# Sums and splits of activations made one stage earlier and kept in DRAM

## Chip, cores and metric

The kernel runs on one core of a Trainium2 chip. The metric is the time of one execution in device microseconds (us); the median of several runs is compared. One execution of each kernel is also recorded by the hardware profiler, and all rows below come from such a record.

## What is computed

The reference is one layer of a flow-matching backbone on 1024 latent tokens and 128 context tokens, 1024 wide. Two parallel mixers come first; the change lies in the channel mixer behind them:

```python
h2 = rmsnorm(x, p["norm2_g"]) * (1.0 + scale2) + shift2
ff = (jax.nn.silu(h2 @ p["w_ffn_gate"]) * (h2 @ p["w_ffn_up"])) @ p["w_ffn_down"]
x = x + gate2 * ff
...
y_prompt = rmsnorm(xp, final_norm_g)
y_sample = rmsnorm(xs, final_norm_g)
```

The hidden width is 2816, that is 22 tiles of 128. The kernel works in float32: each operand of a matmul is split in a high part (a cast to float32r) and a low part (the rest), and a product is the three matmuls high*high, high*low, low*high.

## The kernel before

**Gate and up stage.** A unit (`ffn_unit`) makes the gate (kind "g") or up (kind "u") product of two of the 22 hidden tiles; units g and u of number p belong together (a pair of units, p = 0 to 10). Seven products replace eight (a scheme of Strassen's kind): sums of weight blocks are made on POOL (L1172 to L1174, L1188), each is split by `split` (copy on ACT, L962; low part on POOL, L963), and PE multiplies it with prepared activations TA and TB (L1149). The tokens are two groups, A with five tiles and B with four. PSUM results are combined by ACT and DVE, gate and up are multiplied, and the hidden activations go to the DRAM tensor `ffd` (L1207). Unit 0 runs for group A first, alone, and for group B after pair 2.

**Down stage.** It multiplies the hidden activations (now the contraction) with w_down. Hidden tiles 2m and 2m+1 form tile m, 0 to 10. Block 0 is m = 0, four blocks take m in pairs (1,2) to (7,8), and the last (`std_block`) takes 9 and 10. Blocks up to m = 8 use the seven-product scheme with KEYS P1 to P7; `std_block` makes plain products. For each m the weights (`wd`, L1332) and the raw activations (`fr`, L1318; `raw0` for m = 0) are loaded. `prep` (called once per key) forms sums of them in place (`sub`, L1346, on POOL) and splits both: BT from the weights, AT from the activations (`split2`: copy on ACT, L1308; low part on DVE or POOL, L1309). `prep_std` does it for 9 and 10 without sums. Products are made by `prods` (L1387) into four PSUM banks Z, W, X, Y, which are added to the accumulator ACC by DVE (L1406; the first time copied by ACT, L1404). A bank is used again when it has been added. The prompt's parts (`load_p`, pr, P) go their own way. Prepared A tiles sit in a ring of NA = 10 buffers, raw ones in NFR = 6; `feed` prepares the next key as `step` counts keys as used, up to FA = 10 ahead. At the end come the gate, the residual (`gate_x`, x1), the squares and the final norm.

**Order.** All DMAs are issued by the queue of SP, in one order. The order on each engine is not that of the program text: a scheduler with a simulated timeline takes each instruction as its inputs and buffers are due, and the text's order decides between those that are ready. So the loads and first splits of `raw0`, written behind the loop of units, run in the midst of it (at 907 us). On the chip each engine, and SP's queue, goes strictly in the order so fixed, and a waiting instruction holds all behind it. The pools pA (A tiles, raw tiles) and px (ACC) lie in memory that TA and TB hold until the last gate and up product.

Of the kernel before, what the change touches and what calls it, by code (L numbers as in the profile page):

```python
# [19 lines left out]
NS = 1024  # L20
# [29 lines left out]
NA = 10  # L50
NFR = 6
# [10 lines left out]
def tile_flow_step(ctx: ExitStack, tc: tile.TileContext, a, o):  # L62
# [25 lines left out]
    def f32(ap):  # L88
        return ap.bitcast(F32)
# [1173 lines left out]
    open_sub("B", {z: ps2 for z in "ZWXY"}, pm0, "m0a")  # L1263
    for p in range(1, NF // 2):
        ffn_unit(p, "g", "AB")
        ffn_unit(p, "u", "AB")
        if p == 2:
            ffn_unit(0, "g", "B")
            ffn_unit(0, "u", "B")

# [7 lines left out]
    BLK = [[0]] + [[m, m + 1] for m in range(1, 9, 2)]  # L1278
    STD = [9, 10]
    KEYS = ("P1", "P2", "P6", "P5", "P7", "P4", "P3")  # L1280
# [3 lines left out]
    LO, HI = slice(0, 512), slice(512, 1024)  # L1284
    A0 = pm0.tile([128, 3, 2, 512], F32R, tag="m0b", name="A0")
    raw0 = pgb.tile([128, 2, NS], F32, tag="gb", name="raw0")
# [14 lines left out]
    def a_new(name):  # L1301
        return pA.tile([128, 2, 512], F32R, tag="A", bufs=NA, name=name)

    def b_new(name):
        return ringed("b", [128, 2, 512], F32R, "wh", NWH, "R", NR, name)
# [5 lines left out]

    def load_a(m):
        if m in araw:
            return
        araw[m] = []
        for f in range(2):
            t_ = raw0[:, f] if m == 0 else pA.tile([128, NS], F32, tag="fr", bufs=NFR, name=f"fr{2 * m + f}")
            SY.dma_start(out=t_, in_=ffd[2 * m + f][:, 0:NS])  # L1318
            araw[m].append(t_)
# [15 lines left out]
    def load_raw(m):  # L1335
        load_w(m)
        load_a(m)
        raws[m] = [x[:, h] for x in wraw[m] + araw[m] for h in (LO, HI)]
# [6 lines left out]
    def sub(out, x, y, op=ALU.subtract, eng=None):  # L1345
        (eng or PL).tensor_tensor(out, x, y, op)  # L1346

    def prep(m, ki):
        key = KEYS[ki]
        w0L, w0H, w1L, w1H, a0L, a0H, a1L, a1H = raws[m]  # L1350
        if key == "P6":
            sub(a0H, a0H, a1H, ALU.add)
            sub(w0H, w1H, w0H, eng=V if m in VSUB else PL)
            sub(a0L, a0H, a0L)
            sub(w0L, w0H, w0L, ALU.add, V if m in VSUB else PL)
        if key == "P7":
            sub(a1L, a1L, a0L)
            sub(a0L, a1H, a0L)
        if key == "P5":
            sub(w1L, w1L, w0L)  # L1360
            sub(w0L, w1H, w0L)
        asrc, bsrc = dict(P1=(a0L, w0L), P2=(a1L, w1L), P6=(a0L, w0L), P7=(a0L, w0H),
                          P4=(a1H, w1L), P5=(a0H, w0L), P3=(a1L, w1H))[key]
        if m == 0:
            A = A0[:, ki] if ki < 3 else a_new(f"A0{key}")
            B = wr.tile([128, 2, 512], F32R, tag="wh" if ki < 6 else "ftA", bufs=NWH if ki < 6 else 1, name=f"B0{key}")
        else:
            A, B = a_new(f"A{m}{key}"), b_new(f"B{m}{key}")
        BT[m, key] = split2(B, bsrc, PL if m == 0 else V)
        AT[m, key] = split2(A, asrc, PL if m > 0 and key in ("P2", "P7") else V)  # L1370

    def prep_std(m, ki):
        w0L, w0H, w1L, w1H, a0L, a0H, a1L, a1H = raws[m]
        for (i, j, asrc), (k, n, bsrc) in (
                (((1, 0, a0H), (0, 0, w0L)), ((1, 1, a1H), (1, 0, w1L)),
                 ((0, 0, a0L), (0, 1, w0H)), ((0, 1, a1L), (1, 1, w1H)))[ki],):
            BT[m, (k, n)] = split2(b_new(f"B{m}{k}{n}"), bsrc, V)
            AT[m, (i, j)] = split2(a_new(f"A{m}{i}{j}"), asrc, PL)
# [222 lines left out]
    for m in BLK[1]:  # L1601
        load_a(m)
# [124 lines left out]
```

## Time and profile before

| | us |
|---|---|
| median of 3 runs | 1538.99 (1536.73 to 1542.13) |
| the profiled execution | 1546.39 |
| its span | 1544.3 |
| PE busy in it | 1470.2 (95%) |
| DVE, ACT, POOL busy | 900.0, 568.5, 721.4 |

Times in rows count from the start of the span. Busy time of PE is time in which some matmul is in its pipeline; a matmul's own length (0.39 us for 512 columns) is longer than the distance to the next one. The gate and up stage with both groups runs from about 793 us, the down stage from 1256.5 us, and the last matmul ends at 1527.3 us.

### The profile page before, as it was taken

The numbers are of one execution on the slowest core, as the hardware profiler recorded it, in microseconds if no ns is written. First come the engines' busy times: TensorE is split into PE (matmuls) and PEld (weight loads), VectorE is DVE, ScalarE is ACT, GpSimd is POOL, SyncE is SP. The second block draws the span as 40 slices with busy tenths as digits, with TensorE's granted clock in tenths as the row PEclk, the third lists the DMA queues.
The fourth block names the chain that finished last, engine by engine and source line by source line (L and its number), as shares of the span: only waits on it lengthen the run. The fifth ranks groups of instructions, "written<-read, shape, count | busy, mean of one in ns | idle before, by whom it ended". The sixth has DMA issues, their size and how long they took to land.

```text
span 1544.3 us, 23785 instructions
## 1 busy us (share of the span) xinstructions
PE 1470.2 (95%) x8999; PEld 1317.4 (85%) x8999; DVE 900.0 (58%) x1786; ACT 568.5 (37%) x1096; POOL 721.4 (47%) x658
## 2 busy tenths in 40 slices
PE   6999999999989999998899999999999998999995
PEld 3799998989968779777679999999999997777774
DVE  4557989997255335379952432222222259989978
ACT  6433243343454121354532343232333244333323
POOL 4920000000022111354688679777777785775454
PEclk9999999999989999999899999999999999999998
DMA  8333233232525653455532122221222255222313
GB/s 310 117 124 96 74 109 97 83 111 91 179 66 177 210 160 113 136 205 176 178 114 86 56 99 86 86 78 44 79 86 73 72 182 185 97 85 86 105 52 123
DMA packets 84703, 180.91 MB, mean 117 GB/s; under 512 B 13790, under 2 KB 44127, under 8 KB 84588
## 3 DMA queue, kind: packets, MB, share of 16 engines
q1 hardware_dynamic: 84588, 179.38, 35.1%
q8 instruction: 71, 1.16, 0.3%
q14 instruction: 44, 0.36, 0.1%
HBM read 141.05 MB, written 38.28 MB: 116 GB/s over the span
## 4 chain that ended last, share of the span: by engine, by line
PE 58%; DVE 11%; issue 2%; DMA 2%; POOL 2%; ACT 1%; SPq 0%; DVEq 0%; ACTq 0%; POOLq 0%
PE U L1387 4%; PE p L106 2%; PE p L105 2%; PE p L104 2%; DVE acc L1406 2%; PE ada L155 1%; DVE wh_out L963 1%; PE V L1387 1%; PE o L978 1%; PE o L979 1%; PE o L977 1%; DVE acc L1485 1%; DMA wd<-in_w_d 1%; PE g L272 1%; PE g L273 1%
## 5 line engine op out<-in xcount | busy, mean ns | idle before, releaser
L94 POOL TENSOR_TENSOR wh_glu<-ws_glu,wh_glu 128x512 fp32r<-128x512 f32 x4 | 5.5, 1388 | 340.3 <-ACT wh_glu L93 340.3
L272 PE MATMUL g<-h,wh_g 128*128 128x384 f32 (+1 forms) x432 | 148.0, 343 | 0.0
L271 PE MATMUL g<-h,wh_g 128*128 128x384 f32 (+1 forms) x432 | 148.0, 342 | 0.0
L273 PE MATMUL g<-h,wh_g 128*128 128x384 f32 (+1 forms) x432 | 147.4, 341 | 0.0
L271 PEld LDWEIGHTS g<-h,wh_g 128*128 128x128 f32 x432 | 82.0, 190 | 0.3 <-issue 0.3
L272 PEld LDWEIGHTS g<-h,wh_g 128*128 128x128 f32 x432 | 82.0, 190 | 0.2 <-issue 0.2
L273 PEld LDWEIGHTS g<-h,wh_g 128*128 128x128 f32 x432 | 82.0, 190 | 0.2 <-issue 0.2
L94 POOL TENSOR_TENSOR wh_pj<-ws_pj,wh_pj 128x512 fp32r<-128x512 f32 x16 | 22.1, 1380 | 103.8 <-ACT wh_pj L93 94.2
L963 DVE TENSOR_TENSOR wh_out<-ws_out,wh_out 128x512 fp32r<-128x512 f32 x32 | 33.8, 1072 | 24.6 <-ACT wh_out L962 24.6
L1346 POOL TENSOR_TENSOR wd<-wd,wd 128x512 f32<-128x512 f32 x25 | 37.7, 1517 | 21.7 <-DMA wd<-in_w_d 10.8
L1387 PE MATMUL q<-B,A 128*128 128x512 f32 x192 | 45.7, 394 | 1.1 <-DVE acc L1406 0.9
L963 POOL TENSOR_TENSOR wh_out<-ws_out,wh_out 128x512 fp32r<-128x512 f32 x16 | 21.8, 1371 | 50.6 <-ACT wh_out L962 47.6
L1387 PEld LDWEIGHTS q<-B,A 128*128 128x128 f32 x192 | 35.9, 188 | 10.1 <-DVE acc L1406 1.3
L1406 DVE TENSOR_TENSOR acc<-acc,U 128x1024 f32<-128x1024 f32 x34 | 41.1, 1213 | 2.0 <-PE U L1387 1.6
L923 DVE TENSOR_TENSOR sgc<-sgc,p 128x384 f32<-128x384 f32 x24 | 13.3, 555 | 48.4 <-PE p L106 48.4
L977 PE MATMUL o<-wh_out,m 128*128 128x512 f32 x96 | 36.6, 409 | 4.6 <-ACT scr0b L1059 4.6
L636 DVE TENSOR_TENSOR ta<-X,Sg 128x56 f32<-128x56 f32 (+10 forms) x88 | 39.5, 449 | 1.1
L639 DVE TENSOR_TENSOR X<-X,tb 128x56 f32<-128x56 f32 (+10 forms) x88 | 39.4, 455 | 0.9
L1166 ACT ACTIVATE fsA<-ftA 128x320 f32<-128x320 f32 x33 | 15.6, 471 | 65.4 <-DVE ftA L1185 39.9
L962 ACT CAST wh_out<-ws_out 128x512 fp32r<-128x512 f32 x48 | 28.3, 615 | 30.1 <-PE o L979 20.3
L1346 POOL TENSOR_TENSOR fr<-fr,fr 128x512 f32<-128x512 f32 x24 | 37.4, 1571 | 4.3 <-DMA fr<-ffd 4.3
L978 PE MATMUL o<-wh_out,m 128*128 128x512 f32 x96 | 38.5, 403 | 0.7 <-DVE wh_out L963 0.7
(1664 smaller groups left out, 4600.0 us busy)
## 6 DMA issues: line engine op xcount, KB each, us to landing
wa<-in_w_ada SPq DMA_DIRECT2D x48, 512.0 KB, 5.7
ws_out<-in_w_out SPq DMA_DIRECT2D x24, 512.0 KB, 3.9
wd<-in_w_d SPq DMA_DIRECT2D x22, 512.0 KB, 8.1
ind<-in SPq DMA_DIRECT2D x54, 192.0 KB, 1.9
fr<-ffd SPq DMA_DIRECT2D x20, 512.0 KB, 4.9
ws_g<-in_w_in SPq DMA_DIRECT2D x18, 512.0 KB, 3.5
sgc<-ind SPq DMA_DIRECT2D x48, 192.0 KB, 3.5
ffd<-fsA SPq DMA_DIRECT2D x11, 640.0 KB, 3.1
```

Of the source, the lines that this page charges most:

```text
L104: PE.matmul(ps, w[:, 0, wsl], act[:, 0][asl], start=first, stop=False)
L271: PE.matmul(ps, w[:, 0, wsl], hi, start=first, stop=False)
L272: PE.matmul(ps, w[:, 0, wsl], lo, start=False, stop=False)
L273: PE.matmul(ps, w[:, 1, wsl], hi, start=False, stop=last)
L636: V.tensor_tensor(A, src, Sc[:, 0, lv, gs].unsqueeze(1).unsqueeze(3).to_broadcast(shp), ALU.mult)
L639: V.tensor_tensor(dst, dst, B[:, ::-1], ALU.add)
L963: (eng or PL).tensor_tensor(w[:, 1, :], src, f32(w[:, 0, :]), ALU.subtract)
L977: PE.matmul(p, mc[t][0][:, k, ts_], w[n][:, 0], start=(k == 0), stop=False)
L978: PE.matmul(p, mc[t][0][:, k, ts_], w[n][:, 1], start=False, stop=False)
L1346: (eng or PL).tensor_tensor(out, x, y, op)
L1387: PE.matmul(ps, A[:, va], B[:, vb], start=(first and ti == 0 and i == 0), stop=(last and ti == n - 1 and i == 2), skip_group_check=True)
L1406: V.tensor_tensor(dst, dst, ps, ALU.add)
```

## The change

For tiles m = 0 to 9 the sums and splits of activations are made inside the gate and up stage. `a_steps(m)` loads the two raw tiles back from `ffd` into the buffer "gb" (ra), makes for each key the sums on DVE, the copy of the high part on ACT and the low part on DVE into one of three staging buffers (`stg`, in the buffer "m0b"), and stores both parts to a DRAM tensor `ad[m]`. The steps are handed to the units as hooks, one after each product. Tile 10 stays as it was. In the down stage `load_at` loads a prepared tile of 512 KB from `ad`; `prep` and `prep_std` now prepare only the weights (and tile 10). Five tiles of m = 0 go to buffers that `stg` and `ra` held (A0, A1). The ring of A tiles grows from 10 to 12, that of raw tiles shrinks from 6 to 4. Sums that POOL made are now made by DVE, and so are the low parts that POOL made (P2, P7 and tile 9).

```diff
--- before.py
+++ after.py
@@ -47,8 +47,8 @@
 XBG = 1
 NWA = 4
 NR = 4
-NA = 10
-NFR = 6
+NA = 12
+NFR = 4
 NW2 = 3
 NPT = 2
 NXR = 2
@@ -1261,12 +1261,64 @@
     pst_.release()
     ps2 = open_pool("psF2", space=PSUM)
     open_sub("B", {z: ps2 for z in "ZWXY"}, pm0, "m0a")
+    KEYS = ("P1", "P2", "P6", "P5", "P7", "P4", "P3")
+    LO, HI = slice(0, 512), slice(512, 1024)
+    BLK = [[0]] + [[m, m + 1] for m in range(1, 9, 2)]
+    STD = [9, 10]
+    ad = {m: dram.tile([7 if m < STD[0] else 4, 128, 2, 512], F32, tag=f"ad{m}", name=f"ad{m}")
+          for m in range(STD[1])}
+    stg = pm0.tile([128, 3, 2, 512], F32R, tag="m0b", name="stg")
+    nstg = 0
+
+    def a_steps(m):
+        box = {}
+
+        def start():
+            raw = pgb.tile([128, 2, NS], F32, tag="gb", name=f"ra{m}")
+            for f in range(2):
+                SY.dma_start(out=raw[:, f], in_=ffd[2 * m + f][:, 0:NS])
+            box["a"] = [raw[:, f, h] for f in range(2) for h in (LO, HI)]
+
+        def one(ki):
+            nonlocal nstg
+            a0L, a0H, a1L, a1H = box["a"]
+            if m >= STD[0]:
+                src = (a0H, a1H, a0L, a1L)[ki]
+            else:
+                key = KEYS[ki]
+                if key == "P6":
+                    V.tensor_tensor(a0H, a0H, a1H, ALU.add)
+                    V.tensor_tensor(a0L, a0H, a0L, ALU.subtract)
+                if key == "P7":
+                    V.tensor_tensor(a1L, a1L, a0L, ALU.subtract)
+                    V.tensor_tensor(a0L, a1H, a0L, ALU.subtract)
+                src = dict(P1=a0L, P2=a1L, P6=a0L, P7=a0L, P4=a1H, P5=a0H, P3=a1L)[key]
+            st_ = stg[:, nstg % 3]
+            nstg += 1
+            S.copy(out=st_[:, 0], in_=src)
+            V.tensor_tensor(st_[:, 1], src, f32(st_[:, 0]), ALU.subtract)
+            SY.dma_start(out=ad[m][ki], in_=f32(st_))
+
+        n = 7 if m < STD[0] else 4
+        return [start, no, no] + [lambda ki=ki: one(ki) for ki in range(n)]
+
+    apend = []
+
+    def anext():
+        if apend:
+            apend.pop(0)()
+
     for p in range(1, NF // 2):
-        ffn_unit(p, "g", "AB")
-        ffn_unit(p, "u", "AB")
+        for kind in "gu":
+            ffn_unit(p, kind, "AB", [anext] * 7)
         if p == 2:
             ffn_unit(0, "g", "B")
             ffn_unit(0, "u", "B")
+            apend += a_steps(2) + a_steps(0)
+        elif p < STD[1]:
+            apend += a_steps(p)
+    while apend:
+        anext()
 
 
     ps2.release()
@@ -1275,15 +1327,11 @@
     pTA.release()
     pT.release()
     psp = open_pool("psC", space=PSUM)
-    BLK = [[0]] + [[m, m + 1] for m in range(1, 9, 2)]
-    STD = [9, 10]
-    KEYS = ("P1", "P2", "P6", "P5", "P7", "P4", "P3")
     px = open_pool("px")
     ACC = px.tile([128, 9, D], F32, tag="acc", name="acc")
     pA = open_pool("pA")
-    LO, HI = slice(0, 512), slice(512, 1024)
     A0 = pm0.tile([128, 3, 2, 512], F32R, tag="m0b", name="A0")
-    raw0 = pgb.tile([128, 2, NS], F32, tag="gb", name="raw0")
+    A1 = pgb.tile([128, 2, 2, 512], F32R, tag="gb", name="A1")
     ring = dict(b=0, w=0)
     AT, BT, PT, raws, araw, wraw = {}, {}, {}, {}, {}, {}
     pR = pE = pW = None
@@ -1309,12 +1357,17 @@
         (eng or V).tensor_tensor(w[:, 1], src, f32(w[:, 0]), ALU.subtract)
         return w
 
+    def load_at(m, ki):
+        key = KEYS[ki] if m < STD[0] else ((1, 0), (1, 1), (0, 0), (0, 1))[ki]
+        if (m, key) in AT:
+            return
+        AT[m, key] = (A0[:, ki] if ki < 3 else A1[:, ki - 3]) if m == 0 and ki < 5 else a_new(f"A{m}_{ki}")
+        SY.dma_start(out=f32(AT[m, key]), in_=ad[m][ki])
+
     def load_a(m):
-        if m in araw:
-            return
         araw[m] = []
         for f in range(2):
-            t_ = raw0[:, f] if m == 0 else pA.tile([128, NS], F32, tag="fr", bufs=NFR, name=f"fr{2 * m + f}")
+            t_ = pA.tile([128, NS], F32, tag="fr", bufs=NFR, name=f"fr{2 * m + f}")
             SY.dma_start(out=t_, in_=ffd[2 * m + f][:, 0:NS])
             araw[m].append(t_)
 
@@ -1334,8 +1387,9 @@
 
     def load_raw(m):
         load_w(m)
-        load_a(m)
-        raws[m] = [x[:, h] for x in wraw[m] + araw[m] for h in (LO, HI)]
+        if m == STD[1]:
+            load_a(m)
+        raws[m] = [x[:, h] for x in wraw[m] + araw.get(m, []) for h in (LO, HI)]
 
     def load_p(m):
         pr = pA.tile([128, 2, 128], F32, tag="pr", bufs=2, name=f"pr{m}")
@@ -1347,35 +1401,31 @@
 
     def prep(m, ki):
         key = KEYS[ki]
-        w0L, w0H, w1L, w1H, a0L, a0H, a1L, a1H = raws[m]
+        w0L, w0H, w1L, w1H = raws[m]
         if key == "P6":
-            sub(a0H, a0H, a1H, ALU.add)
             sub(w0H, w1H, w0H, eng=V if m in VSUB else PL)
-            sub(a0L, a0H, a0L)
             sub(w0L, w0H, w0L, ALU.add, V if m in VSUB else PL)
-        if key == "P7":
-            sub(a1L, a1L, a0L)
-            sub(a0L, a1H, a0L)
         if key == "P5":
             sub(w1L, w1L, w0L)
             sub(w0L, w1H, w0L)
-        asrc, bsrc = dict(P1=(a0L, w0L), P2=(a1L, w1L), P6=(a0L, w0L), P7=(a0L, w0H),
-                          P4=(a1H, w1L), P5=(a0H, w0L), P3=(a1L, w1H))[key]
+        bsrc = dict(P1=w0L, P2=w1L, P6=w0L, P7=w0H, P4=w1L, P5=w0L, P3=w1H)[key]
         if m == 0:
-            A = A0[:, ki] if ki < 3 else a_new(f"A0{key}")
             B = wr.tile([128, 2, 512], F32R, tag="wh" if ki < 6 else "ftA", bufs=NWH if ki < 6 else 1, name=f"B0{key}")
         else:
-            A, B = a_new(f"A{m}{key}"), b_new(f"B{m}{key}")
+            B = b_new(f"B{m}{key}")
+        load_at(m, ki)
         BT[m, key] = split2(B, bsrc, PL if m == 0 else V)
-        AT[m, key] = split2(A, asrc, PL if m > 0 and key in ("P2", "P7") else V)
 
     def prep_std(m, ki):
-        w0L, w0H, w1L, w1H, a0L, a0H, a1L, a1H = raws[m]
-        for (i, j, asrc), (k, n, bsrc) in (
-                (((1, 0, a0H), (0, 0, w0L)), ((1, 1, a1H), (1, 0, w1L)),
-                 ((0, 0, a0L), (0, 1, w0H)), ((0, 1, a1L), (1, 1, w1H)))[ki],):
-            BT[m, (k, n)] = split2(b_new(f"B{m}{k}{n}"), bsrc, V)
-            AT[m, (i, j)] = split2(a_new(f"A{m}{i}{j}"), asrc, PL)
+        w0L, w0H, w1L, w1H = raws[m][0:4]
+        (k, n), bsrc = (((0, 0), w0L), ((1, 0), w1L), ((0, 1), w0H), ((1, 1), w1H))[ki]
+        if m == STD[1]:
+            a0L, a0H, a1L, a1H = raws[m][4:8]
+            ij, asrc = (((1, 0), a0H), ((1, 1), a1H), ((0, 0), a0L), ((0, 1), a1L))[ki]
+            AT[m, ij] = split2(a_new(f"A{m}_{ki}"), asrc, PL)
+        else:
+            load_at(m, ki)
+        BT[m, (k, n)] = split2(b_new(f"B{m}{k}{n}"), bsrc, V)
 
     def bank(z, name):
         return psp.tile([128, 2, 512], F32, tag=z, name=name)
@@ -1598,8 +1648,9 @@
     for ki in range(7):
         prep(0, ki)
     load_w(1)
-    for m in BLK[1]:
-        load_a(m)
+    for ki in range(4):
+        for m in BLK[1]:
+            load_at(m, ki)
     load_p(0)
     for st_ in last_st:
         SY.dma_start(**st_)
```

## Rows read from the trace of the kernel before

**Rows 1.** Stages: stretch, length, busy us (count) of PE, PEld, DVE, ACT, POOL, clock...
```profile
850.00:1256.50 406.50, 406.50 (x3099) 406.50 (x3099) 105.92 (x220) 125.46 (x252) 305.00 (x260) 1.00 0.22 75
...
1256.50:1527.30 270.80, 257.12 (x1085) 203.92 (x1083) 247.30 (x249) 102.66 (x192) 167.16 (x103) 0.99 0.34 117
...
1527.30:1544.30 17.00, 0.00 (x0) 0.00 (x0) 11.97 (x29) 5.62 (x15) 5.22 (x4) 0.64 0.38 153
```

**Rows 2.** PE alone in a stretch of the down stage without a gap.
```profile
1338.50:1363.50 25.00, 25.00 (x110) 1.00 0.43 153
```

**Rows 3.** Waits of PE, 1240 to 1545: total us, times, longest; 11 rows.
```profile
PE Zp L1387 <- DVE acc L1406: 3.4, 4, 1.4
...
PE V L1387 <- DVE acc L1406: 2.5, 1, 2.5
...
PE Y L1387 <- DVE B1P L1309: 1.6, 1, 1.6
```

**Rows 4.** PE's timeline after a wait: start, length, instruction, count, idle before.
```profile
1466.89 1.29 PE L1387 MATMUL V<-B7P,A7P 128*128 128x512 f32 x3 [2.49 <-DVE acc L1406]
...
1471.32 0.86 PE L1387 MATMUL U<-B7P,A7P 128*128 128x512 f32 x3
```

**Rows 5.** Chain of waits in the down stage: start, length, what.
```profile
1323.10 0.60 DVE A3P L1309
...
1323.70 1.70 DVE A4P L1309
...
1330.88 1.70 DVE A4P L1309
...
1333.76 3.06 PE Zp L1387 x12
...
1376.87 1.79 POOL fr L1346 x2
...
1382.31 1.27 DVE B5P L1309
```

**Rows 6.** Raw activations fr, 1256.5 to 1480: busy us (count) of DVE, ACT, POOL.
```profile
1256.50:1480.00 223.50, 40.33 (x40) 38.93 (x64) 87.74 (x56) 0.98 0.38 130
```

**Rows 7.** Timeline of DVE and POOL where both have work.
```profile
1412.41 1.75 POOL L1346 TENSOR_TENSOR fr<-fr 128x512 f32<-128x512 f32 x1
...
1412.92 1.78 DVE L1309 TENSOR_TENSOR A8P<-fr,A8P 128x512 fp32r<-128x512 f32 x1
...
1414.11 1.74 POOL L1346 TENSOR_TENSOR wd<-wd 128x512 f32<-128x512 f32 x1
```

**Rows 8.** All engines, 1266 to 1276; the last number is GB/s.
```profile
1266.00:1276.00 10.00, 9.07 (x40) 7.14 (x38) 10.00 (x9) 8.54 (x15) 10.00 (x7) 1.00 1.04 412
```

**Rows 9.** Timeline of POOL before unit g3 and before unit g9.
```profile
898.05 1.29 POOL L1172 TENSOR_TENSOR s_g3AB<-ws_g3AB 128x512 f32<-128x512 f32 x1 [1.39 <-DMA ws_g3AB<-in_w_g]
...
904.00 2.54 POOL L963 TENSOR_TENSOR wh_g3ABs<-ws_g3AB,wh_g3ABs 128x512 fp32r<-128x512 f32 x2
...
1153.90 1.30 POOL L963 TENSOR_TENSOR wh_g9ABa<-ws_g9AB,wh_g9ABa 128x512 fp32r<-128x512 f32 x1
```

**Rows 10.** Timeline of PE in unit g3 and in unit g9.
```profile
906.22 1.63 PE L1149 MATMUL WAg3AB<-TA,wh_g3ABs 128*128 128x320 f32 x10
...
1167.77 1.93 PE L1149 MATMUL ZAg9AB<-TA,wh_g9ABa 128*128 128x320 f32 x12
```

**Rows 11.** Timeline of SP's queue at the gate and up stage's end.
```profile
1173.53 19.02 SPq L957 DMA_DIRECT2D ws_g10AB<-in_w_g  x2
...
1217.91 22.47 SPq L1332 DMA_DIRECT2D wd<-in_w_d  x3
...
1256.72 1.75 SPq L1318 DMA_DIRECT2D fr<-ffd  x4
...
1263.19 2.77 SPq L1332 DMA_DIRECT2D wd<-in_w_d  x2
```

**Rows 12.** Timeline of DVE in the last block.
```profile
1498.67 0.69 DVE L1406 TENSOR_TENSOR acc<-acc,qp 128x512 f32<-128x512 f32 x1 [2.81 <-PE qp L1387]
```

## The prediction

> **What bounds the kernel now.** I first read the stretches by stage. In the gate and up stage (850 to 1256.5 us) PE is busy without a gap, while POOL is busy for 305 of 406.5 us and DVE for 106. In the down stage (1256.5 to 1527.3) DVE is busy for 247 of 270.8 us and PE has gaps; behind it lies a tail of 17 us without a matmul [rows 1]. So the stage that the work leaves is short of DVE, and the one that it enters is short of PE.
>
> How much the gaps cost is read from PE's pace. In an unbroken stretch of the down stage 110 matmuls start in 25 us, 0.2273 us each [rows 2]. The code makes 99 matmuls in the first block, 192 in each of four blocks and 216 in the last, 1083 together; at that pace they need 246.2 us. The stage takes 270.8, so **24.6 us** are lost, and that is the ceiling of what this stage can give back. The list of PE's waits names 13.7 us of it in 11 rows, and nearly all end on DVE: an accumulation of an earlier product (L1406) or a split of a weight tile (L1309) [rows 3]. The other 10.9 us are what a wait drags behind it: after the 2.5 us wait that ends at 1466.89, the next 12 matmuls take until 1471.32, 4.43 us instead of 2.73 [rows 4].
>
> The chain of waits then shows what DVE was doing in front of those waits. Splits of activation tiles (A3P, A4P) lie directly before the accumulation for which PE's Zp waits at 1333.76, and at 1376.87 POOL's sums of activations (fr, L1346) lie before B5P's split at 1382.31, on which U waits [rows 5]. This is the work that is moved.
>
> **What leaves the down stage.** On the raw activations, the stretch to 1480 has 40 DVE splits (40.3 us), 64 ACT copies (38.9) and 56 POOL instructions (87.7) [rows 6]. Tile 10 keeps its 4 copies and 4 POOL splits. So DVE loses 40, and four more of tile 0 at the same mean of 1.01, 44 us; POOL loses 52 at 1.57, 81 us; ACT loses 60 and four at 0.61, 39 us. DVE falls from 247 to 203 us of 270.8 by that alone. It falls further because its remaining splits meet POOL less often: one split takes 0.60 us in the chain and the next 1.70 [rows 5], and where both engines work without pause they take turns, POOL starting every 1.70 us (1412.41, 1414.11) with a DVE split between [rows 7].
>
> What that is worth: the rows of PE's waits split into 3.9 us before 1291 (the first U wait, Xp, and Y on B1P) and 9.8 after. Of the later ones I take 85%, **8.3 us**, since each has a moved instruction or its contention ahead of it; what stays are Zp's waits when one DVE instruction is in the way. Of the first 3.9 I take **1.5**, because that place gets a new load, below. Of the 10.9 us behind waits I take half, **5.4**. The ends are 0 and 24.6 us; I take 15.2, nearer the upper end, because the engine behind the waits loses about a quarter of its work.
>
> **What enters the gate and up stage.** 67 copies on ACT at 0.61 (41 us on an engine with 125 of 406.5 busy [rows 1, 6]); on DVE 67 splits and 36 sums, 103 instructions, of which a free one takes 0.60 and one between POOL's 1.70, so 62 to 175 us on top of 106: it fits. On SP 20 loads and 67 stores of 0.5 MB, nine a pair of units, 106 GB/s on top of 75 [rows 1]; the same queue moved 412 GB/s [rows 8].
>
> The price is paid by POOL, which makes the weight splits that feed PE. A POOL split alone takes 1.30 us [rows 9], in turn with DVE 1.70, so each moved DVE instruction costs POOL up to 0.4 us. At most 12 fall in a pair of units, which takes 44.4 us (SP's loads for the next g unit stand at 1173.53 and 1217.91 [rows 11]): 4.9 us. POOL is busy for three quarters of the stage [rows 1], 33.3 of 44.4 us in a pair, so it would reach 38.2 and still fit. The Trainium skill, "SBUF — State Buffer", section "SBUF: two separate sides", speaks against this change: a DVE instruction with two SBUF inputs and a GpSimd one hold the shared port pair exclusively and the loser fully blocks. By that rule the whole 0.6 us of each of the 103 would be added to POOL, 62 us instead of 41; the rows show 0.4, and the evacuations now in this stage read PSUM, so no row of the stage itself shows it.
>
> Whether that reaches PE is a matter of the lead. The split for g9's first product starts at 1153.90, its matmul at 1167.77: 13.9 us of lead [rows 9, 10]. A pair's 4.9 us is inside that lead. One place has none: after the second half of unit 0, POOL comes from the first sum of g3 at 898.05 to the splits of two tiles from 904.00, and PE uses the first of the low parts at 906.22, not a microsecond after it is done [rows 9, 10]. There tiles 2 and 0 are now prepared in the same microseconds; seven POOL instructions lie in that chain, at 0.4 each 2.8 us. I put **3 us** on it, between 0 (the order moves them behind) and 8 (the whole chain and SP wait too).
>
> On SP the added stores wait for DVE, and behind them stand the weight loads. SP already stands for most of 22.47 us on a buffer at 1217.91 [rows 11]; a store late by some us is hidden by the same 13.9 us of lead. If that lead is gone, each us is PE's.
>
> **The start of the down stage.** The new loads of prepared tiles into pA come when the last matmul of the stage before ends, as the raw loads do now at 1256.72, and the weight tiles of block 1 stand behind them, now issued up to 1263.19 [rows 11]. Before: four raw tiles, 2.1 MB. After: ten tiles, 5.2 MB, then 1.3 MB of stores and prompt parts and 1.6 MB of weights; 8.1 MB at 412 GB/s [rows 8] is 19.7 us, so block 1's weights land near 1278. PE finishes block 0's 99 matmuls at 0.2273 near 1279. It is just in time, hence the small 1.5 us above, with ends of 3.9 gained and 6 lost. The Trainium skill, "DMA: Bandwidth & Descriptors", Specifications, gives about 358 GB/s of HBM per core; at that figure they would land near 1281 and cost 2 us more, but the row shows 412, so the row decides. Later blocks need 14 tiles and four weights, 9.4 MB in 192 x 0.2273 = 43.6 us, 216 GB/s, half of that.
>
> **The tail** stays. DVE last waits for PE at 1498.67 (2.81 us) [rows 12] and then works through to the end, so whatever PE gains before comes through and the last 46 us keep their length.
>
> **Sum.** 15.2 gained, 3 lost: 12.2. The profiled execution took 1546.4 us (span 1544.3), so 1534.2; it was 7.4 above the median of 1539.0, and 12.2 off the median gives **1527**.
>
> **Rivals.** *The start is bound by transfers*: if all twelve buffers and raw tile 10 are loaded ahead of block 1's weights, 2.1 MB more are in front, 5 us, and the 1.5 gained there go too: 1534. For it: 412 GB/s is already held from 1266 to 1276 [rows 8]. Against: the weights stand earlier in the program than tile 10.
>
> *The waits on accumulation are PE's own order*: it takes turns over four banks, and a wait on L1406 (9.7 of 13.7 us) may stay with DVE at two thirds. Then only waits on splits and a share behind them go, some 4 us against 3 lost: 1538. Against it: unbroken stretches of 25 us [rows 2].
>
> *Slower, by POOL in the gate and up stage*: POOL's idle quarter is partly waiting for ACT's copies and may not be usable. The lead then shrinks with each of eight pairs; from 1.9 us lost a pair (15.2 / 8) the change loses. At half of the 4.9 us unhidden and the whole lead used up, 2.5 us in eight pairs is 20: 1544; with SP's stores late as well 1560. I put 1548. For it: the rule of the SBUF page, and POOL's 75%. Against: 11 us idle a pair and 13.9 of lead.
>
> *It doesn't do what it says*: tiles 8 and 9 are prepared so late that the first five tiles, which reuse the buffers of that preparation, are loaded after PE wants them. Five tiles are 2.6 MB, 6.4 us, with a store's round trip before, some 10 to 12 us of stall: 1538. Against: tile 9 can start at 1218 and needs only four splits.
>
> **How the numbers follow.** Forecast 0.52, transfers 0.15, accumulation 0.13, slower 0.12, late tiles 0.08. About 0.3% (4.6 us) is what a measurement can tell from no change, so faster means under 1534.4: 0.50 of the forecast, half of the transfers and a little of the others, 0.61; slower is over 1543.6: 0.12 and parts of late tiles and the forecast, 0.16; the rest 0.23. The range goes from 1517, where nearly the whole 24.6 us come back and little is lost, to 1546, inside the slower case.
>
> **What the profile will show.** Right: the down stage near 256 us with DVE at or under 200, few waits on L1406, POOL's weight splits in the gate and up stage over 1.30 us and PE still without gaps there except near 905. Wrong: gaps in g or u products on POOL's splits; a wait on B1P or B2P near 1280 longer than 2 us; matmuls of the first block that wait for a DMA.

## The result and the profile after

The changed kernel takes **1550.09 us** at the median (1546.81 to 1553.36, 6 runs) against 1540.27 for the kernel before, measured beside it; the ratio is 1.0066 with a 95% interval of 1.0047 to 1.0085. It is slower by some 10 us, where 12 us faster was forecast. Its profiled execution took 1548.89 us, with a span of 1547.1. (One of the twelve executions of wd_first, below, ran at a granted clock of 0.75 and took 1794.72 us; its median counts that execution, its ratio does not.)

Three stretches can be compared between any two executions: from the first matmul of ZAg2 (pair 2's start) to the first U matmul of the down stage, from there to the start of the last qp matmul (the blocks), and from there to the end (the tail). The time that the work ahead of pair 2 takes varies from one execution to the next by itself: pair 2 starts at 837.5 us in the profiled execution of the kernel before, and at 829.2 in a second one of the same kernel ("before again", below), which is 8 of the 9 us by which their spans differ (1544.3 and 1535.2). So the second is used for comparison.

The stretches of the kernel before (second execution) and of the changed one; the columns are those of [rows 1]:

```profile
829.20:1248.20 419.00, 419.00 (x3194) 419.00 (x3193) 108.60 (x226) 128.83 (x258) 314.92 (x269) 1.00 0.23 78
1248.20:1489.20 241.00, 228.16 (x963) 180.84 (x962) 219.42 (x207) 89.41 (x158) 149.57 (x94) 0.99 0.36 123
```
```profile
830.70:1265.00 434.30, 423.24 (x3195) 420.77 (x3194) 204.66 (x326) 155.60 (x321) 318.94 (x260) 1.00 0.50 186
1265.00:1495.50 230.50, 223.55 (x963) 179.23 (x962) 152.62 (x163) 56.59 (x97) 62.56 (x43) 1.00 0.61 223
1495.50:1547.10 51.60, 30.42 (x124) 23.90 (x122) 44.38 (x71) 18.95 (x48) 30.74 (x17) 0.84 0.30 112
```

The gate and up part grew by **15.3 us** (419.0 to 434.3), the blocks shrank by **10.5** (241.0 to 230.5), and the tail grew by **5.6** (46.0 to 51.6): +10.4, against 9.8 between the medians. PE, without a gap in the first stretch before, now works 423 of 434 us there.

**Gate and up.** The list of PE's waits in that stretch is empty for the kernel before. After, it has ten rows, 11.1 us in all; the other 4.2 of the 15.3 are PE's own busy time, 423.24 us instead of 419.00. Total us, times, longest; the first four:

```profile
PE XBg9AB L1149 <- DVE fstB L1182: 1.8, 1, 1.8
PE XBu0B L1149 <- DVE fstB L1182: 1.6, 1, 1.6
PE YAg4AB L1149 <- DVE ftA L1185: 1.4, 1, 1.4
PE YAg6AB L1149 <- DVE ftA L1185: 1.4, 1, 1.4
```

None names POOL's weight splits. All name DVE's evacuation of a PSUM bank: PE may not write X or Y again before DVE has taken the last product out. What ACT and DVE stood on in the same stretch:

```profile
ACT stg L1298 <- DMA ra<-ffd: 58.9, 17, 7.7
ACT ftA L1176 <- POOL fsA L1168: 34.0, 7, 5.7
...
DVE stg L1299 <- ACT stg L1298: 61.0, 19, 8.6
DVE ftA L1179 <- ACT ftA L1176: 42.7, 12, 6.4
```

The new copy of a raw tile (ra) on ACT waited 58.9 us in all for the tile to land, and DVE's low part behind it 61.0 us for that copy. One such place, unit g6, in SP's, ACT's, DVE's and PE's timelines (start, length, instruction, count, idle before it and what ended that):

```profile
1040.69 0.38 SPq L1207 DMA_DIRECT2D ffd<-fstB  x1
...
1045.12 0.81 SPq L1279 DMA_DIRECT2D ra<-ffd  x2
...
1039.44 1.93 PE L1149 MATMUL XAg6AB<-TA,wh_g6ABs 128*128 128x320 f32 x12
...
1041.46 0.49 DVE L1182 TENSOR_TENSOR ftA<-ftA,XAg6AB 128x320 f32<-128x320 f32 x1
...
1049.09 0.62 ACT L1298 CAST stg<-ra 128x512 fp32r<-128x512 f32 x1 [6.98 <-DMA ra<-ffd]
1049.75 1.30 DVE L1299 TENSOR_TENSOR stg<-ra,stg 128x512 fp32r<-128x512 f32 x1 [7.80 <-ACT stg L1298]
1050.98 0.41 DVE L1182 TENSOR_TENSOR fstB<-fstB,XBg6AB 128x256 f32<-128x256 f32 x1
1051.44 1.67 PE L1149 MATMUL XBg6AB<-TB,wh_g6ABa 128*128 128x256 f32 x12 [0.56 <-DVE fstB L1182]
...
1053.87 0.48 DVE L1185 TENSOR_TENSOR ftA<-ftA,YAg6AB 128x320 f32<-128x320 f32 x1
1054.49 2.00 PE L1149 MATMUL YAg6AB<-TA,wh_g6ABs 128*128 128x320 f32 x12 [1.38 <-DVE ftA L1185]
```

SP issues the last store of hidden activations at 1040.69 and the load of the same data at 1045.12; in between it issues one load of weights and then stands on that store (16.6 us in ten such waits in this stage). The tile is used at 1049.09: 8.4 us for the round trip through DRAM. The split stands in ACT's and DVE's fixed order right behind the evacuation of XA, which comes at once (its product, begun at 1039.44, takes 1.93 us), and right ahead of those of XB and YA. DVE idles from 1041.95 to 1049.75, the evacuations behind it come late, and PE stops.

How much lateness PE can bear is in unit u6 of the kernel before. PE's products of bank XA, and DVE's evacuation between them:

```profile
1063.15 1.93 PE L1149 MATMUL XAu6AB<-TA,wh_u6ABs 128*128 128x320 f32 x12
1066.33 1.93 PE L1149 MATMUL YAu6AB<-TA,wh_u6ABs 128*128 128x320 f32 x12
1072.66 1.93 PE L1149 MATMUL XAu6AB<-TA,wh_u6ABa 128*128 128x320 f32 x12
...
1065.12 0.49 DVE L1182 TENSOR_TENSOR ftA<-ftA,XAu6AB 128x320 f32<-128x320 f32 x1 [1.27 <-PE XAu6AB L1149]
```

The bank is free at 1065.61 and wanted at 1072.66: a lead of **7.05 us**. In g6 of the kernel before, the two banks on which PE stops here have 7.42 (XB) and 7.06 us (YA). DVE's stand of 7.80 us is longer than that.

**Tail.** The ring of raw tiles ("fr", 6 buffers before, now 4) also holds residual tiles x of the end. SP and POOL of the changed kernel, then POOL of the kernel before:

```profile
1466.40 31.92 SPq L1529 DMA_DIRECT2D x<-x1d  x4
...
1493.18 4.75 POOL L1536 TENSOR_TENSOR acc<-acc,x 128x1024 f32<-128x1024 f32 x2 [1.16 <-DVE acc L1535]
1499.27 2.67 POOL L1536 TENSOR_TENSOR acc<-acc,x 128x1024 f32<-128x1024 f32 x1 [1.34 <-DMA x<-x1d]
```
```profile
1476.76 5.74 POOL L1486 TENSOR_TENSOR acc<-acc,x 128x1024 f32<-128x1024 f32 x2 [2.74 <-DMA x<-x1d]
1483.68 2.40 POOL L1486 TENSOR_TENSOR acc<-acc,x 128x1024 f32<-128x1024 f32 x1 [1.18 <-DMA x<-x1d]
```

Four x loads take SP 31.92 us, since it stands 30.2 us, in three waits, on sums of POOL that hold the buffers. Sums that POOL had made before the last matmuls now fall beside DVE's final chain, where DVE's smallest instructions wait for POOL: first after, then before.

```profile
1499.60 2.35 DVE L132 TENSOR_SCALAR r_6v<-sst 128x2 f32<-128x2 f32 x1
1506.64 2.33 DVE L137 TENSOR_SCALAR r_6t<-r_6t 128x2 f32<-128x2 f32 x1
```
```profile
1501.54 0.17 DVE L132 TENSOR_SCALAR r_6v<-sst 128x2 f32<-128x2 f32 x1
1506.38 0.17 DVE L137 TENSOR_SCALAR r_6t<-r_6t 128x2 f32<-128x2 f32 x1
```

These two alone are 4.3 us of the 5.6.

### The profile page after: what moved, and what is told of

It is laid out like the page before. It is cut to its first block, busy times and chain, and to the rows that moved or that the text cites. A ratio compares the mean times of both kernels' runs of the same rounds, so it can differ in the third digit from the quotient of the medians.

```text
span 1547.1 us, 24049 instructions
## 1 busy us (share of the span) xinstructions
PE 1465.0 (95%) x8999; PEld 1312.0 (85%) x8999; DVE 937.4 (61%) x1842; ACT 563.2 (36%) x1096; POOL 641.7 (41%) x602
## 3 DMA queue, kind: packets, MB, share of 16 engines
q1 hardware_dynamic: 103884, 249.64, 45.9%
## 5 line engine op out<-in xcount | busy, mean ns | idle before, releaser
L1299 DVE TENSOR_TENSOR stg<-ra,stg 128x512 fp32r<-128x512 f32 x67 | 74.4, 1122 | 61.0 <-ACT stg L1298 61.0
L1298 ACT CAST stg<-ra 128x512 fp32r<-128x512 f32 x67 | 41.2, 618 | 91.1 <-DMA ra<-ffd 58.9
L963 DVE TENSOR_TENSOR wh_out<-ws_out,wh_out 128x512 fp32r<-128x512 f32 x32 | 33.8, 1071 | 24.6 <-ACT wh_out L962 24.6
L963 POOL TENSOR_TENSOR wh_out<-ws_out,wh_out 128x512 fp32r<-128x512 f32 x16 | 21.9, 1373 | 50.6 <-ACT wh_out L962 47.6
L962 ACT CAST wh_out<-ws_out 128x512 fp32r<-128x512 f32 x48 | 28.3, 615 | 30.2 <-PE o L979 20.3
```

Of the source, the lines that this page charges most:

```text
L963: (eng or PL).tensor_tensor(w[:, 1, :], src, f32(w[:, 0, :]), ALU.subtract)
L1298: S.copy(out=st_[:, 0], in_=src)
L1299: V.tensor_tensor(st_[:, 1], src, f32(st_[:, 0]), ALU.subtract)
```

## The experiments

**Theory L** (late tile): the gate and up part loses because the raw tile lands later than the fixed order assumes, and ACT and DVE stand ahead of evacuations. **Theory P** (the prediction's rival): moved DVE instructions slow POOL, whose weight splits become late. **Theory R**: the tail loses by the ring of four. The stretches of all kernels, from the starts of the same three matmuls, and the time for which ACT or DVE (the larger of the two) stood on the landing of ra in the first of them (us):

| kernel | gate and up | blocks | tail | sum | stood on ra |
|---|---|---|---|---|---|
| before again | 419.0 | 241.0 | 46.0 | 706.0 | - |
| changed | 434.3 | 230.5 | 51.6 | 716.4 | 58.9 |
| other_raw | 436.1 | 230.9 | 51.7 | 718.7 | 62.7 |
| gated | 422.1 | 234.8 | 51.7 | 708.6 | 12.0 |
| raw5 | 437.4 | 230.3 | 46.0 | 713.7 | 59.2 |
| gated_raw5 | 420.4 | 235.5 | 46.0 | 701.9 | 11.9 |
| double_low | 457.2 | 234.3 | 46.2 | 737.7 | 16.8 |
| steps_only | 436.8 | 243.1 | 45.9 | 725.8 | 62.6 |
| down_only_raw5 | 419.0 | 229.4 | 46.3 | 694.7 | - |
| wd_first | 422.3 | 232.5 | 46.1 | 700.9 | 13.1 |
| extra_one | 442.3 | 237.3 | 46.1 | 725.7 | 18.4 |
| later_raw5 | 438.3 | 234.4 | 46.0 | 718.7 | 64.0 |
| tie_only | 439.3 | 232.6 | 46.0 | 717.9 | 43.9 |

**before_again**: the kernel before, once more.

> The kernel before, profiled a second time. The sum started from one profiled execution of 1546.4 us in which PE's waits of the down stage come to 13.7 us, while the median is 1540.3. Theory A: the waits belong to every execution, and the 6 us lie in all stages alike; then PE's waits from 1240 us on come to 12 to 15 us again. Theory B: that execution had more waits than a usual one; then a span near 1538 goes with waits of some 8 us, and the down stage could never give back what I took. Ratio 1.000.

1540.17 us, ratio 1.000 (0.9984 to 1.0016). PE's waits of the down stage recur (13.1 us from 1240 us on), so [rows 3] was no accident of one execution. Theory A missed one thing: the difference does not lie in all stages alike, 8 us of it lie ahead of pair 2.

**other_raw**: the steps load tile m-1, stored one pair earlier.

> The changed kernel, but the steps of tile m (m from 2 on) load the raw activations of tile m-1, which were stored a pair of units earlier: the sums, splits and stores are as many, only the wait for the store just made falls away (so it computes with wrong activations). Theory A, the queue: in the gate and up stage DVE and ACT stand in their order before the first split of each tile until the raw tile has landed, and the evacuations behind them come late; without that wait PE has no gaps there, the down stage begins near 1257 instead of 1265, and the time is 1541 to 1543. Theory B, the port: the 103 added DVE instructions and POOL's splits hold each other up; then nothing changes, 1549 to 1551, with PE's waits for DVE of some 11 us left.

```diff
-                SY.dma_start(out=raw[:, f], in_=ffd[2 * m + f][:, 0:NS])
+                SY.dma_start(out=raw[:, f], in_=ffd[2 * (m - (m > 1)) + f][:, 0:NS])
```

1549.41 us, ratio 1.006 (1.0041 to 1.0079). A miss as a test: the loads kept their place in SP's order behind the same stores, ACT still stood 62.7 us on the landing, and the loss stayed. The load was issued 4.4 us behind the last store (1045.26 to 1049.63), as before, though it no longer reads what that store wrote; so the run does not show that the dependence is what holds it. Two of PE's waits here, 1.8 and 0.7 us, name the weight split of g3 (ACT's copy and POOL's low part), at the place that the prediction had marked.

**gated**: the right data; before a tile's first split DVE adds 0 times a later evacuation result to one column of ra (two instructions a tile), which ties the split behind that evacuation, and four empty steps instead of two lie between load and split.

> The changed kernel with the right data; before the first split of each tile DVE adds zero times a value of a later evacuation of the running unit to one column of the raw tile, and one more hook is left empty behind the load, so that the order of DVE and ACT puts the splits behind that evacuation. Theory A, the queue: the splits then stand where the raw tile has landed, PE's waits for DVE in the gate and up stage fall from 11 us to under 3, and the time is 1541 to 1544. Theory B, the port: 1549 to 1551 as before, since the same instructions run.

```diff
+        def gate():
...
+            for f in range(2):
+                V.scalar_tensor_tensor(q[:, f], tmp["A"][0:1, 0, 0:2, 0:1], 0.0, q[:, f], ALU.mult, ALU.add)
...
+            if ki == 0:
+                gate()
...
-        return [start, no, no] + [lambda ki=ki: one(ki) for ki in range(n)]
+        return [start, no, no, no, no] + [lambda ki=ki: one(ki) for ki in range(n)]
```

1537.9 us, ratio 0.9994 (0.998 to 1.0008), below the 1541 to 1544 expected. (The expectation names one more empty step, the edit leaves two.) With every moved instruction still there, the gate and up part loses 3.1 us instead of 15.3. This is for theory L: the instructions as such are not the loss, their place is. Medians and stretches agree only to some us: the sum is 2.6 us above that of before again, the median 2.2 below the 1540.06 measured beside it.

**raw5**: five raw buffers instead of four.

> The changed kernel with five buffers for raw tiles and x1 instead of four (before: six). Theory A: the tail is 5.6 us longer than before (51.4 against 45.8 us from DVE's last long wait for PE on) because SP waits for a buffer from 1466 on, the x1 tiles land late, and POOL's additions fall into DVE's last chain; with five buffers POOL's additions begin before 1486 again and the time is 1545 to 1547. Theory B: the tail is longer since PE arrives there earlier and DVE's order is another; then 1549 to 1551.

```diff
-NFR = 4
+NFR = 5
```

1548.01 us, ratio 1.0053 (1.0034 to 1.0073). The tail is 46.0 us, to the tenth that of the kernel before: theory R. Its gate and up part drew 437.4 us, so the median gained only 2 and lies between the two forecasts.

**gated_raw5**: both edits.

> Both suspected causes undone together: the first split of each prepared tile is tied to a later point of the program (a sum with 0 times a later evacuation result, and two more empty steps), and the ring of raw tiles holds five instead of four. If the two causes are the late raw tile in ACT's and DVE's queues and the ring, their effects add: gate and up stage 422 us as in the run with the later split alone, blocks of the down stage 231 to 235, tail 46.0; 699 to 703 us from the first g2 matmul to the end against 706 to 707 of the kernel before, so 1533 to 1536 us at the median, 4 to 7 below before. If the moved DVE instructions on POOL's port cost anything worth naming, or the down stage gains nothing in the end, it stays at 1540.

1536.96 us, ratio 0.9989 (0.9974 to 1.0003). The stretches add up as expected (701.9 us); the median is a microsecond above what was expected and not told from the kernel before. In the first stretch one wait of PE is left, 0.5 us.

```profile
830.90:1251.30 420.40, 419.86 (x3194) 419.28 (x3193) 220.38 (x346) 156.73 (x319) 323.21 (x259) 1.00 0.53 192
...
PE ZBg0B L1149 <- ACT fstB L1176: 0.5, 1, 0.5
```

**double_low**: each low part of a moved split made twice on DVE.

> As gated_raw5, but each low part of the 67 moved splits is made twice on DVE, the second into the same place: 67 more DVE instructions of 0.6 to 1.7 us beside POOL's weight splits, nothing else. If POOL loses up to 0.4 us to each moved DVE instruction and its lead over PE is used up (the rival of the prediction), the gate and up stage grows by 10 to 27 us over that of gated_raw5. If the lead covers it, and only the order of the queues had cost time, it stays within 3 us of gated_raw5, with POOL's busy time in that stage higher.

```diff
             V.tensor_tensor(st_[:, 1], src, f32(st_[:, 0]), ALU.subtract)
+            V.tensor_tensor(st_[:, 1], src, f32(st_[:, 0]), ALU.subtract)
```

1570.1 us, ratio 1.0196 (1.0175 to 1.0217), 36.8 us more in the gate and up part than gated_raw5. "Within 3 us" was plainly wrong, so DVE's time there is not free, and the 10 to 27 us of the other forecast were too few. But theory P's way is not what the rows show: one wait of 0.8 us names a POOL split; nearly all the others name evacuations on DVE and ACT. POOL can still have a part in it by another way: ACT's copies out of PSUM stand 40.8 us on POOL's product fsA (L1168), against 18.0 in gated_raw5.

```profile
828.20:1285.40 457.20, 430.47 (x3194) 425.41 (x3193) 287.51 (x413) 153.80 (x319) 335.74 (x259) 0.99 0.48 177
...
PE ZBg0B L1149 <- ACT fstB L1176: 4.3, 1, 4.3
PE XAg5AB L1149 <- DVE ftA L1182: 4.3, 1, 4.3
PE ZAu7AB L1149 <- ACT fsA L1166: 2.8, 1, 2.8
PE XAu8AB L1149 <- DVE ftA L1182: 2.2, 1, 2.2
...
PE WAg4AB L1149 <- POOL wh_g4ABs L963: 0.8, 1, 0.8
```

**extra_one**: the 67 extra DVE instructions with one SBUF input.

> As gated_raw5, with 67 more DVE instructions as in double_low, at the same places, but with one SBUF input (a multiplication by 1.0 into the place of the low part, ahead of the real one) instead of two. double_low lost 36.8 us in the gate and up stage (457.2 against 420.4). If what counts is DVE's time in front of the evacuations (3.17 us a product, of which evacuations take 0.91), the loss goes with the time these instructions take: at 0.35 to 0.7 us each instead of 1.13 some 10 to 25 us. If it is the contention of two-input DVE instructions with POOL, the loss is under 5 us and POOL's instructions are no longer than in gated_raw5 (323 us busy).

```diff
+            V.tensor_scalar(st_[:, 1], src, 1.0, None, ALU.mult)
             V.tensor_tensor(st_[:, 1], src, f32(st_[:, 0]), ALU.subtract)
```

1557.11 us, ratio 1.0116 (1.0095 to 1.0136).

```profile
829.70:1272.00 442.30, 425.05 (x3194) 421.00 (x3193) 258.92 (x413) 155.28 (x319) 328.67 (x259) 1.00 0.50 183
...
L1308 DVE TENSOR_SCALAR stg<-ra 128x512 fp32r<-128x512 f32 x67 | 49.3, 747 | 5.6 <-DMA ad<-stg 5.4
```

DVE is busy 38.5 us more than in gated_raw5 and the stretch is 21.9 longer; in double_low it was 67.1 and 36.8. That is 0.57 and 0.55 us per us of DVE: the loss goes with DVE's time. Contention is not excluded as a part of it: POOL grew by 5.5 and 12.5 us, a quarter to a third of the loss, and the one-input instruction was no control without contention, since it took 0.41 us at the shortest and 1.53 at the longest.

What room DVE has is an estimate from these rows: a product takes 3.17 us (1063.15 to 1072.66 are three), two evacuations 0.49 + 0.42, which leaves 2.26. In gated_raw5 a tile's seven splits (79.7 / 67 = 1.19) and four sums (1.13) are 12.9 us in seven products, 1.84 each: just inside. With the second low part they are 2.25 a split and 20.5 us a tile, 2.9 each, and in extra_one 1.84 and 17.7 us, 2.5 each: both outside.

**steps_only**: all the new work in the gate and up part, but tiles 1 to 10 are summed and split again in the down stage as before.

> The entry alone: the gate and up stage makes all sums, splits and stores as in the changed kernel, but the down stage of tiles 1 to 10 loads raw activations and makes its own sums and splits as before, with the rings of before (10 prepared, 6 raw). Only tile 0 still comes prepared. If the loss lies in the entry: gate and up stage +15 us over before (434 us from the first g2 matmul), the blocks at 238 to 242, tail 46: 1550 to 1556 us. If the loss lies in the down stage's exchange of raw for prepared tiles, it is at 1540 to 1543.

```diff
-NA = 12
-NFR = 4
+NA = 10
+NFR = 6
...
+        if m > 0:
+            asrc = dict(P1=a0L, P2=a1L, P6=a0L, P7=a0L, P4=a1H, P5=a0H, P3=a1L)[key]
+            AT[m, key] = split2(a_new(f"A{m}{key}"), asrc, PL if key in ("P2", "P7") else V)
```

1556.74 us, ratio 1.0101 (1.0078 to 1.0124): at the upper end of what was expected: the entry alone costs 17.8 us in its stretch, and nothing is gained.

**down_only_raw5**: the exit alone. 

> The exit alone: no steps in the gate and up stage; the down stage loads halves of raw tiles where the changed kernel loads prepared ones (as many bytes, from the earlier activations; the sums and splits of the activations of tiles 0 to 9 are left out, so the output is not that of the reference), with a raw ring of five. It is the ceiling of this change: gate and up stage 419 us as before, blocks 230 to 231, tail 46.0, 695 to 696 us from g2 on against 706 to 707: 1528 to 1530 us, 10 to 12 below before. If the shorter down stage of the changed kernel only took back what its longer gate and up stage had pushed out (other work done early), the blocks stay at 238 to 241 and the time is at 1538 to 1540. The prediction's 15.2 us would give 1525.

```diff
-            apend += a_steps(2) + a_steps(0)
-        elif p < STD[1]:
-            apend += a_steps(p)
...
-        SY.dma_start(out=f32(AT[m, key]), in_=ad[m][ki])
+        SY.dma_start(out=f32(AT[m, key]), in_=ffd[2 * m + ki % 2][:, 0:NS].rearrange("p (v c) -> p v c", v=2))
```

1529.6 us, ratio 0.9939 (0.9918 to 0.996). As expected, the blocks give back 11.6 us, not 15.2: that is the most that this change can gain with its loads in this order.

**wd_first**: gated_raw5 loses 6 of these 11.6 us again in block 0. There SP issues five loads of prepared tile 0 ahead of two weight tiles, the first of which is tile 0's second half, and ACT waits for it (rows of gated_raw5):

```profile
1229.83 4.00 SPq L1374 DMA_DIRECT2D A<-ad  x5
1234.82 1.59 SPq L1394 DMA_DIRECT2D wd<-in_w_d  x2
...
1242.50 0.62 ACT L1365 CAST B0P<-wd 128x512 fp32r<-128x512 f32 x1 [6.20 <-DMA wd<-in_w_d]
...
1260.45 3.06 PE L1446 MATMUL U<-B0P,A 128*128 128x512 f32 x12 [3.36 <-ACT acc L1463]
```

> As gated_raw5, but the five loads of prepared tile 0 wait until the second weight tile of tile 0 has landed (five one-element sums on POOL write into their buffers from that weight tile). In gated_raw5 these loads are issued at 1229.83, the two weight tiles at 1234.82 behind them, POOL stands 6.50 us at 1242.55 on their landing, and PE stands 3.36 us at 1260.45 for ACT's copies of the accumulators. If the order of these loads is what block 0 loses, the blocks go from 235.5 us to 230 to 232, the sum from the first g2 matmul to the end from 701.9 to 696 to 699: 1531 to 1534 us. If the waits of block 0 have another cause (POOL late by its own work), it stays at 1537.

```diff
     load_raw(0)
+    lastw = wraw[0][1][0:1, 0:1]
+    for ki in range(3):
+        PL.tensor_tensor(A0[0:1, ki, 0, 0:1], lastw, lastw, ALU.add)
+    for ki in range(2):
+        PL.tensor_tensor(A1[0:1, ki, 0, 0:1], lastw, lastw, ALU.add)
```

1534.77 us, ratio **0.9961 (0.9946 to 0.9977)**: faster than both kernels (1538.2 for the kernel before beside it), 15 us below the changed one. The 3.36 us wait is gone (0.4 left) and the blocks are at 232.5 us; the gate and up part drew 422.3, so the sum is 700.9 instead of the 696 to 699 expected, and the median lies above the 1531 to 1534.

**later_raw5**: four empty steps without the tie.

> The changed kernel with a ring of five raw tiles and four empty steps instead of two between a raw tile's load and its first split, without the sum that ties the split to a later evacuation. It tells the two edits of gated_raw5 apart. If ACT's wait for the late raw tile is only a matter of how many products lie between, gate and up stage 421 to 424 us and 1536 to 1539. If the planner still orders the splits by its own, earlier, landing time, ACT keeps waiting on the load (about 60 us in all) and it is at 1545 to 1549 as raw5.

1547.51 us, ratio 1.0061 (1.0044 to 1.0079). The distance alone changes nothing: in g6 DVE's order is that of raw5, with the first split between the evacuations of XA and XB, so the scheduler placed it by its own landing time and not by the empty steps.

```profile
ACT stg L1298 <- DMA ra<-ffd: 64.0, 17, 7.8
```

**tie_only**: wd_first with two empty steps.

> wd_first with two empty steps, as in the changed kernel, instead of four: of the two edits that undo the loss in the gate and up stage only the tie of the first split to a later evacuation is left. If the tie alone sets the order (four empty steps without it gave 438.3 us in that stage), it is at 420 to 424 us with no wait of ACT on the landing of the raw tile, 1533 to 1537 at the median. If the distance counts as well, ACT or DVE stand on the raw tile for 30 us or more in all and the stage is at 428 or above: 1541 or more.

1548.93 us, ratio 1.007 (1.0045 to 1.0095). The tie alone isn't enough either, the second of the two cases: tied to an evacuation two products earlier, it still comes ahead of the landing. Two products are 6.3 us; the stands are up to 8.7.

```profile
DVE ra L1287 <- DMA ra<-ffd: 43.9, 9, 8.7
```

Read down the table's last column: with 44 to 64 us of standing on ra the gate and up part takes 434 to 439 us, with 12 to 13 it takes 420 to 422. The two exceptions are the kernels with more DVE work, where standing on ra is not what costs the time. Theory L holds for the changed kernel, with theory R for the tail.

## Why the prediction was wrong

- **The gate and up part: 3 us predicted, 15.3 measured.** This is the step that turned the sign. "It fits" was worked out from totals (ACT 41 us more, DVE 62 to 175) and not from places. Two things were missed. The lead of 13.9 us [rows 9, 10] belongs to POOL's weight splits; the moved work stands in ACT's and DVE's order among evacuations of PSUM banks, whose lead is 7.05 us. And for the moved step's load no landing was priced: it follows a store of the same data through DRAM, 8.4 us later. The prediction has SP wait for DVE's stores; that ACT and DVE would stand on a load was not in it. Its sign (PE without gaps there except near 905) failed in units g4 to g9.
- **POOL's port.** 41 us more on POOL were predicted, hidden by the lead. POOL's same 198 instructions for weights (L963 and L1172 to L1188) take 255.6 us before again and 273.2 in gated_raw5: 17.6. They were hidden, as said: no wait of PE in the changed kernel names POOL's splits, though their lead over g9's first product, 13.9 us from the split's start in [rows 9, 10], was down to 6.6 (1165.68 to 1172.27). The place near 905 us, for which the 3 us stood, did lose time, 1.6 us at 895.43, but on an evacuation by DVE. The dearer side was DVE's: its 67 splits in gated_raw5 took 1.19 us on the mean against 0.67 at the shortest (the 0.60 of [rows 5] is a step of a chain). The Trainium skill, "SBUF — State Buffer", section "SBUF: two separate sides", says that the loser fully blocks; the prediction's estimate by that reading was 62 us on POOL. The rows agree that both sides pay, but POOL paid 17.6.
- **SP.** The 67 stores were said to be hidden by the lead; no weight load appears among the gate and up part's waits of PE. Right for PE.
- **The down stage: 15.2 predicted, 10.5 measured, 11.6 at most** (down_only_raw5). The mechanism was right: DVE falls from 219.4 to 152.6 us, and the waits on L1406 that made up 9.7 of the 13.7 us in [rows 3] are down to a few of about 0.4 to 0.9 us. What a wait drags behind it was there too, and more of it than was taken: 12.9 us of named waits in before again became 7.0, and 10.5 came back, 1.8 per us, as in 24.6 / 13.7, where the prediction's 15.2 stood on 9.8 of named waits, 1.55 per us. Mis-sized was how many named waits go: 9.8 predicted, 5.9 gone. What stays is at the start of the stage.

```profile
PE Y L1437 <- DVE B1P L1357: 2.3, 1, 2.3
PE U L1437 <- ACT acc L1454: 1.4, 2, 0.9
PE Zp L1437 <- ACT acc L1454: 1.1, 1, 1.1
```

- **The start of the stage.** "Just in time" failed by the sign the prediction had set for it, a wait on B1P over 2 us: block 1's weights are issued at 1274.91, behind ten loads of prepared tiles and the prompt's stores, and PE waits 2.3 us, until 1300.10, where it had waited 1.6 [rows 3]. The transfer is not what came last, though: ACT's copy of the weight tile, held 1.85 us by its landing, begins at 1296.32, and DVE makes the low part at 1299.36, behind an accumulation for which it stood on PE until 1297.62.
- **The tail: no change predicted, 5.6 measured.** The change of NFR from 6 to 4 stood in the diff and got no term. The argument that DVE works through to the end [rows 12] held only while POOL's sums of x lay ahead of that chain.
- **The rivals.** "Slower by the POOL port" gave 1548, near the 1550 measured, but for another reason: its mechanism, POOL's lead shrinking with each pair until it is gone, isn't in the rows: the lead over the first g product is 6.6 us in g5 (980.75 to 987.34) and still 6.6 in g9. None of the rivals was the one that came.

How PE's 11.1 us of waits in the gate and up part divide is in the trace of the changed kernel. A rival to the stand on ra is the lateness of POOL's fsA ahead of ACT's copies (34.0 us of waits; 3.0 before, 18.0 in gated_raw5). But in units g4 to g9 DVE takes XA out 0.1 to 1.0 us after its product, so that lateness is made up by then; XB, behind the stand on ra, follows 7.1 to 9.4 us after its product and YA 8.3 to 9.8. Nine of the ten waits, 9.5 us, are on these two banks. The tenth, 1.6 us on XBu0B, is DVE's own time: it works without a pause from 886.42 until it has taken XB out at 895.38, with moved splits and sums ahead of that.

Left open: what fsA's lateness costs in the two kernels with more DVE work (40.8 us of ACT's waits in double_low, 36.1 in extra_one), and whether it is the dependence on the store or only the place in SP's order that makes ra late; other_raw was to tell, and did not.

## What to carry to other kernels

Work moved into a stage with idle engines has to be priced at its place in each engine's order: ask what the first moved instruction waits for (here a store and load through DRAM), what stands behind it, and the lead of the tightest resource that those instructions free, PSUM banks as well as weights. Every buffer count in a diff needs a term of its own, with all users of that ring. Where a fixed order rests on an assumed landing time, look for the consumer's stand on the load; here, tying the consumer behind a later event and leaving it distance brought the gate and up part to within 1.4 to 3.3 us of the kernel before, and either by itself did not.

## What the runs showed of the hardware

- A store of hidden activations, the load that depends on it and its first use, through SP's one queue, took 8.4 us (1040.69 to 1049.09): 4.4 from the store's issue to the load's (1040.69 to 1045.12, with one other load between), and 4.0 from there to the use. In other_raw the load was issued 4.4 us behind the store as well, though it read data stored a pair earlier.
- A DVE instruction on 128x2 elements took 0.17 us alone and up to 2.35 beside POOL's sums of 128x1024 (2.4 us each).
- DVE instructions on 128x512 with one SBUF input took 0.75 us on the mean beside POOL (0.41 to 1.53), those with two 1.09 (0.67 to 1.78), in the same kernel (extra_one). POOL's time grew by 5.5 us there, and by 12.5 in double_low.
